# Two 256-column matmuls in place of a 512-column one in the weight-stationary products, and two feature tiles in a PSUM bank

## The chip, the cores and the metric

The kernel runs on one core of one Trainium2 chip. The metric is the device time of the program in microseconds, the median of the timed runs. The profile is one execution, taken by the hardware profiler on that core.

## The reference

A two-layer trunk over 256 tokens of width 2048, all in float32. Layer 0 is gated linear attention and a squared-ReLU MLP, layer 1 is stick-breaking attention over one shared K/V and another such MLP. Cut to what matters here:

```
h = x                                              # (256, 2048)
h = h + gla_mixer(rms_norm(h), ...)                # proj = x @ w_in: q, k (1024 each), v, r (2048 each), a_low (16)
h = h + sq_relu_mlp(rms_norm(h), w_up0, w_down0)   # square(relu(x @ w_up)) @ w_down, 2048 -> 8192 -> 2048
k, v = rms_norm(h) @ kv_w                          # 512 each
h = h + stick_breaking(rms_norm(h) @ w_q, k, v) @ w_out
h = h + sq_relu_mlp(rms_norm(h), w_up1, w_down1)
return rms_norm(h)
```

Every product with a weight matrix is kept close to float32 accuracy by splitting both sides in a high part and a rest (both float32r) and adding three partial products: high by high, rest of the tokens by high weights, high tokens by the rest of the weights.

## The kernel before, in words

**Weights.** `plan` lists all weight units of 1 MB in the order of use. `prefetch` loads one unit into `raw` (pool `wraw`, three buffers, issued from SP) and splits it half by half: ScalarE casts the high part `wh` (L147), VectorE takes the difference `wl` (L148), both into pool `wsp`, three buffers of each. `next_half` keeps three halves ready. A half holds eight k tiles of 128x128 for a weight-stationary product.

**Two forms of product.** Token-stationary products (`half_n`, L202 to L204: the down projections `dn`, `op`, `v`, `r`, `sv`) hold 128 tokens still and move 512 weight columns. Each is three matmuls of 512 columns, with stationaries that are slices of an activation tile (`hT`, `oT`, `xg`, `xkv`). Weight-stationary products (`unit_t`, L160 to L182: `up`, `qk`, `sk`, `sq`, `alow`) hold a 128x128 block of weights still and move the tokens. An activation tile has, for each of the 16 k tiles, 512 columns: 256 high and 256 rest, side by side. For each k tile (a block, below) `unit_t` issues two matmuls into one bank of pool `psB` (two banks): L169 moves all 512 columns against `wh`, so that high by high lands in columns 0 to 255 and rest by high in columns 256 to 511, and L172 moves the 256 high columns against `wl` into columns 0 to 255. The low one stands ahead of the high one, but for the first k tile.

**Finishing a unit.** `joined` (L185 to L188) copies columns 256 to 511 of the bank to SBUF on ScalarE and adds them to the others on VectorE. The MLP then takes the squared ReLU on VectorE (L562), and splits the result into `hT`: ScalarE the high part (L563), VectorE the rest (L564). All that is 256 columns wide.

**Order.** The MLP goes through four quarters of the 8192 features: 16 `up` units, then four column chunks of `dn` over the same features. `hT` is in pool `actp` for the quarters 0 and 2 and in `actc` for 1 and 3 (L556). Engines take their instructions in program order. Attention work (scores, outputs) stands in generators and is handed out by `pump` after every half of a product, so that its small matmuls lie between the blocks.

Of the kernel before, what the change touches and what calls it, by code (L numbers as in the profile page):

```python
# [8 lines left out]
F32 = mybir.dt.float32  # L9
# [4 lines left out]
ALU = mybir.AluOpType  # L14
# [25 lines left out]
def yoco_kernel(ctx: ExitStack, tc: tile.TileContext, a: dict):  # L40
    nc = tc.nc
    V, S, PE = nc.vector, nc.scalar, nc.tensor

    # one table set serves every function used here
    S.preload_act_table_set("natural_log_exp_and_others")
# [23 lines left out]

# [1 line left out]
    pending = []  # L71
# [10 lines left out]

    # the first n given out so far have to be complete
    def drain(n=None):
# [6 lines left out]

    # ---- weights: every unit is loaded whole, then split in halves, exactly, into a
    # 12-bit part and the rest; splits are issued ahead of the products that use them ----
    def out_order(w):
# [27 lines left out]
    def prefetch():  # L122
        i = state["n"]
        if i == 2 * len(plan):
            return
        state["n"] += 1
        if i % 2 == 0:
            for todo in before.pop(i // 2, []):
                todo()
            raw = wraw.tile([P, 2048], F32, tag="raw", name="raw")  # L130
            for lo, hi in ((0, 512), (512, 1024), (1024, 2048)) if i == 0 else ((0, 2048),):
                nc.sync.dma_start(raw[:, lo:hi], plan[i // 2][:, lo:hi])
                for todo in between.pop((i, hi), []):
                    todo()
            state["raw"] = raw
        part = state["raw"][:, (i % 2) * 1024:(i % 2 + 1) * 1024]
        last = i - 2 * len(plan) + 8
        if last < 0:
            wh = wsp.tile([P, 1024], F32R, tag="wh", name="wh")
            wl = wsp.tile([P, 1024], F32R, tag="wl", name="wl")  # L140
        else:
            # the last chunk's products come one token tile after the other: all its weights stay
            if last == 0:
                state["stay"] = [act_tile(n).rearrange("p k t -> p (k t)") for n in ("stay_h", "stay_l")]
            wh, wl = [b[:, last * 1024:(last + 1) * 1024] for b in state["stay"]]
        for lo, hi in ((0, 512), (512, 1024)) if i == 0 else ((0, 1024),):
            S.copy(wh[:, lo:hi], part[:, lo:hi])  # L147
            V.tensor_tensor(wl[:, lo:hi], part[:, lo:hi], wh[:, lo:hi].bitcast(F32), op=ALU.subtract)  # L148
        ready.append((wh, wl))
# [8 lines left out]

    # out[feature, token]: weights stationary, [high | low] tokens moving
    def unit_t(act, name, steps=1):  # L160
        ps = psB.tile([P, 512], F32, tag="psB", name=name)
        for kt in range(KT):
            if kt % 8 == 0:
                wh, wl = next_half()
            o = (kt % 8) * P
            first, last = kt == 0, kt == KT - 1

            def high():
                PE.matmul(ps, wh[:, o:o + P], act[:, kt, :], start=first, stop=last)  # L169

            def low():
                PE.matmul(ps[:, 0:T], wl[:, o:o + P], act[:, kt, 0:T], start=False, stop=False)  # L172

            if first:
                high()
                low()
            else:
                low()
                high()
            if kt % 8 == 7:  # L180
                pump(steps)
        return ps  # L182

    # sum of the two halves of a bank
    def joined(ps, out, rows=P):  # L185
        lo = t256("lo")
        S.copy(lo[0:rows], ps[0:rows, T:2 * T])  # L187
        V.tensor_tensor(out, ps[0:rows, 0:T], lo[0:rows], op=ALU.add)  # L188

    # out[token, column chunk]: tokens stationary, weights moving  # L190
    def banks(name):
# [24 lines left out]

    # a tile as the sum of two that the tensor engine takes in one pass
    def split(src, tile):
# [12 lines left out]

    # 1 / sqrt(u), one Newton step behind the tables
    def rsqrt(u, out):
# [9 lines left out]

# [1 line left out]
    ident = const.tile([P, P], F32, name="ident")  # L245
# [20 lines left out]

# [1 line left out]
    xg = act_tile("xg")  # L268
# [48 lines left out]

    # a value per token, from partitions to the free axis of all partitions
    def spread(col, out, scale):
# [6 lines left out]

    # transposed, scaled and split: what the next products read
    def feed(c, targets):
# [29 lines left out]

# [1 line left out]
    oT = act_tile("oT")  # L360

    # scores of one head: decayed queries and keys, level by level; every exponent is at most 0
    def scores(hd, qT, kT, st, sx):
# [21 lines left out]

        # between the two token tiles, and on the diagonal
        e = t512("e0").rearrange("p (f t) -> p f t", f=2)
# [19 lines left out]

        # within them: keys of a pair's first half against queries of its second
        for lv, s in enumerate(LEVELS):
# [30 lines left out]

    # outputs of one head, its norm, the gate
    def outputs(hd, st, sx, vv, gs):
# [42 lines left out]

    # the output gate times the head's gain
    def gates(pss):
# [14 lines left out]
    def queries_keys():  # L502
        qT = g512("qk", 4, "qT").rearrange("p (f t) -> p f t", f=2)
        kT = g512("qk", 4, "kT").rearrange("p (f t) -> p f t", f=2)
        for dst in (qT, kT):
            for f in range(2):
                joined(unit_t(xg, "qk"), dst[:, f])
        return qT, kT

    for hd in range(GLA_H):  # L510
        st = [half.tile([P, P], F32, tag=f"st{t}", name=f"st{t}", bufs=1) for t in range(NT)]
        sx = half.tile([P, P], F32, tag="sx", name="sx", bufs=1)
        if hd == 0:
            pv, pr = banks("v"), banks("r")
            for kg in range(4):
                unit_n(pv, xg, kg)
                unit_n(pr, xg, kg)
            qT, kT = queries_keys()
            drain()
            vv = values(pv)  # L520
            gs = gates(pr)
            araw = t256("araw")
            spread(rstd0, rbc0, 1.0)
            joined(unit_t(xg, "alow"), araw[0:16], rows=16)
            V.tensor_tensor(alow, araw[0:16], rbc0[0:16], op=ALU.mult)
            give(scores(hd, qT, kT, st, sx))
        else:
            qT, kT = queries_keys()
            give(scores(hd, qT, kT, st, sx))
            vv = values(chunk_n(xg, "v"))  # L530
            gs = gates(chunk_n(xg, "r"))
# [22 lines left out]
    def mlp(act, rstd2, ssq, after, last=None):  # L554
        for q in range(NQ):
            hT = act_tile("hT", actc if q % 2 else actp)  # L556
            for f in range(KT):
                ps = unit_t(act, "up")
                s = t256("s")
                joined(ps, s)  # L560
                y = t256("y")
                V.scalar_tensor_tensor(y, s, 0.0, s, op0=ALU.max, op1=ALU.mult)  # L562
                S.copy(hT[:, f, 0:T], y)  # L563
                V.tensor_tensor(hT[:, f, T:2 * T], y, hT[:, f, 0:T].bitcast(F32), op=ALU.subtract)  # L564
            for c in range(NCH):
# [39 lines left out]

# [1 line left out]
    rstd, _ = squared_rstd(ssq, "rstd2")  # L607
# [3 lines left out]
    kvs = const.tile([P, 2048], F32, tag="kvs", name="kvs")  # L611
    for n in range(KVH):
        joined(unit_t(xkv, "sk"), kvs[:, n * T:(n + 1) * T])
    ps = chunk_n(xkv, "sv")
# [19 lines left out]

    # one group of heads; keys on partitions, (head, query) along the free axis
    def sticks(n, qs):
        heads = slice(n * GRP, (n + 1) * GRP)

        # scores of a key tile against a query tile
        def score(qt, kt):  # L640
# [11 lines left out]

        # softplus, split: the products below have a side of ones and zeros
        def soft(z):
# [7 lines left out]

        # less everything between the key (itself too) and the query
        def weigh(z, own, later=None):
# [45 lines left out]
    for n in range(KVH):  # L710
        qs = [t512(f"q{t}") for t in range(NT)]
        for g in range(GRP):
            ps = unit_t(xq, "sq", 1 + (len(pending) > 1 or g == GRP - 1))
            s = t256("s")
            joined(ps, s)
            for t in range(NT):
                V.tensor_tensor(qs[t][:, g * P:(g + 1) * P], s[:, t * P:(t + 1) * P],
                                rbc[:, t * P:(t + 1) * P], op=ALU.mult)
        give(sticks(n, qs))
# [45 lines left out]

# ---- layouts: stationary units [feature tile][partition][k tile, 128], moving units
# [1 line left out]
def _stationary(w):  # L768
# [17 lines left out]
def _lay_out(i):  # L786
# [27 lines left out]
    r["final_g"] = np.ascontiguousarray(i["final_g"])  # L814
    # constants of the shapes alone
    r["ident"] = np.eye(P, dtype=np.float32)
# [27 lines left out]
```

## Time and profile before

| what | value |
|---|---|
| device time, median of 3 runs | 2115.25 us (2115.14 to 2115.3) |
| profiled execution, first to last instruction | 2113.3 us |
| TensorE matmul busy | 2097.4 us, 99% of the span |
| weight loads on TensorE | 1763.1 us, 83% |
| VectorE busy | 1313.0 us, 62% |
| ScalarE busy | 1039.5 us, 49% |
| DMA read | 384.58 MB, 183 GB/s over the span |

The profile gives no other time of its own execution than the span; the runs are some 2 us longer than it. A matmul's row has a start that is recorded and an end that is modelled, so durations of consecutive matmuls overlap; how long one holds the engine is read from start to start. A weight load (PEld) belongs to each matmul and runs beside the matmul ahead of it.

### The profile page before, as it was taken

Reading aid. Unit: us, or ns where it says so; the run is one execution under the profiler, and the core shown is the slowest. Engines: PE = TensorE matmul, PEld = TensorE weight load, DVE = VectorE, ACT = ScalarE, POOL = GpSimd, SP = SyncE. Lnnn points to the kernel's source line nnn. Section 1 sums busy time; section 2 is a strip of 40 time slices with the busy share of each in tenths; the row PEclk is TensorE's granted clock in tenths of the full one; section 3 lists DMA queues with packets and bytes.
Section 4 is the critical chain, followed back from the end, with each engine's and each line's share of the span. In section 5 each row is a group of like instructions: output and inputs, shape, how many; then the busy total and the mean of one; then the engine's idle time right before and its main releaser. Section 6 shows DMA issues by size and latency. Waiting matters only on the chain.

```text
span 2113.3 us, 26650 instructions
## 1 busy us (share of the span) xinstructions
PE 2097.4 (99%) x10544; PEld 1763.1 (83%) x10544; DVE 1313.0 (62%) x1804; ACT 1039.5 (49%) x1447; POOL 0.2 (0%) x4
## 2 busy tenths in 40 slices
PE   8999999999999999999999999999999999999998
PEld 7888888888888888888888888888888888888886
DVE  5767876665566556556666687666556546655655
ACT  5645655544344344434455487544344434434443
POOL 0000000000000000000000000000000000000000
PEclk9999999999999999999999999999999999999999
DMA  8544444555555555555555644455555555555553
GB/s 313 180 160 160 156 164 157 182 180 188 192 194 183 188 191 181 197 189 190 182 182 178 216 142 156 165 188 188 193 187 190 187 186 192 181 197 185 193 182 137
DMA packets 55741, 388.40 MB, mean 184 GB/s; under 512 B 6448, under 2 KB 6960, under 8 KB 9152
## 3 DMA queue, kind: packets, MB, share of 16 engines
q1 hardware_dynamic: 55616, 386.70, 53.3%
q8 instruction: 83, 1.36, 0.3%
q14 instruction: 42, 0.34, 0.0%
HBM read 384.58 MB, written 2.10 MB: 183 GB/s over the span
## 4 chain that ended last, share of the span: by engine, by line
PE 98%; DVE 0%; ACT 0%; DMA 0%; SPq 0%; issue 0%; DVEq 0%
PE up L169 23%; PE up L172 11%; PE dn L204 11%; PE dn L203 11%; PE dn L202 11%; PE sq L169 3%; PE op L204 3%; PE op L202 3%; PE op L203 3%; PE qk L169 3%; PE sq L172 1%; PE r L202 1%; PE r L204 1%; PE r L203 1%; PE v L204 1%; PE v L202 1%
## 5 line engine op out<-in xcount | busy, mean ns | idle before, releaser
L148 DVE TENSOR_TENSOR wl<-raw,wh 128x1024 fp32r<-128x1024 f32 (+1 forms) x715 | 874.6, 1224 | 593.2 <-ACT wh L147 580.7
L147 ACT CAST wh<-raw 128x1024 fp32r<-128x1024 f32 (+1 forms) x715 | 751.2, 1051 | 725.9 <-PE dn L203 392.0
L169 PE MATMUL up<-xm,wh 128*128 128x512 f32 x2048 | 714.7, 398 | 0.0
L172 PE MATMUL up<-xm,wl 128*128 128x256 f32 x2048 | 554.5, 281 | 0.0
L169 PEld LDWEIGHTS up<-xm,wh 128*128 128x128 f32 x2048 | 376.8, 188 | 84.0
L172 PEld LDWEIGHTS up<-xm,wl 128*128 128x128 f32 x2048 | 386.8, 189 | 10.8
L204 PE MATMUL dn<-wl,hT 128*128 128x512 f32 x992 | 390.3, 393 | 0.0
L203 PE MATMUL dn<-wh,hT 128*128 128x512 f32 x992 | 389.0, 392 | 0.0
L202 PE MATMUL dn<-wh,hT 128*128 128x512 f32 x992 | 387.5, 391 | 0.0
L203 PEld LDWEIGHTS dn<-wh,hT 128*128 128x128 f32 x992 | 186.2, 188 | 42.6
L202 PEld LDWEIGHTS dn<-wh,hT 128*128 128x128 f32 x992 | 186.2, 188 | 41.3
L204 PEld LDWEIGHTS dn<-wl,hT 128*128 128x128 f32 x992 | 186.2, 188 | 40.8
L187 ACT COPY lo<-up 128x256 f32<-128x256 f32 x128 | 47.7, 373 | 227.6 <-PE up L169 227.6
L188 DVE TENSOR_TENSOR s<-up,lo 128x256 f32<-128x256 f32 x128 | 54.4, 425 | 118.4 <-ACT lo L187 118.4
L202 PE MATMUL op<-wh,oT 128*128 128x512 f32 x256 | 101.1, 395 | 0.0
L203 PE MATMUL op<-wh,oT 128*128 128x512 f32 x256 | 101.0, 395 | 0.0
L204 PE MATMUL op<-wl,oT 128*128 128x512 f32 x256 | 100.7, 394 | 0.0
L169 PE MATMUL sq<-xq,wh 128*128 128x512 f32 x256 | 91.0, 396 | 0.0
L169 PE MATMUL qk<-xg,wh 128*128 128x512 f32 x256 | 90.5, 397 | 0.0
L172 PE MATMUL qk<-xg,wl 128*128 128x256 f32 x256 | 69.9, 283 | 0.0
L172 PE MATMUL sq<-xq,wl 128*128 128x256 f32 x256 | 69.4, 280 | 0.0
L202 PE MATMUL v<-wh,xg 128*128 128x512 f32 x128 | 51.7, 404 | 6.3 <-ACT wh L147 6.3
(206 smaller groups left out, 1838.2 us busy)
## 6 DMA issues: line engine op xcount, KB each, us to landing
raw<-in_w_up SPq DMA_DIRECT2D x128, 1024.0 KB, 4.9
raw<-in_w_down SPq DMA_DIRECT2D x128, 1024.0 KB, 4.9
raw<-in_w_r SPq DMA_DIRECT2D x16, 1024.0 KB, 4.9
raw<-in_w_out SPq DMA_DIRECT2D x16, 1024.0 KB, 4.8
raw<-in_w_sq SPq DMA_DIRECT2D x16, 1024.0 KB, 4.8
raw<-in_w_so SPq DMA_DIRECT2D x16, 1024.0 KB, 5.0
raw<-in_w_v SPq DMA_DIRECT2D x15, 1024.0 KB, 4.9
raw<-in_w_q SPq DMA_DIRECT2D x8, 1024.0 KB, 4.9
```

The source lines that it names most:

```text
L147: S.copy(wh[:, lo:hi], part[:, lo:hi])
L148: V.tensor_tensor(wl[:, lo:hi], part[:, lo:hi], wh[:, lo:hi].bitcast(F32), op=ALU.subtract)
L169: PE.matmul(ps, wh[:, o:o + P], act[:, kt, :], start=first, stop=last)
L172: PE.matmul(ps[:, 0:T], wl[:, o:o + P], act[:, kt, 0:T], start=False, stop=False)
L187: S.copy(lo[0:rows], ps[0:rows, T:2 * T])
L188: V.tensor_tensor(out, ps[0:rows, 0:T], lo[0:rows], op=ALU.add)
L202: PE.matmul(pss[t], xl, wh[:, o:o + CH], start=kt == 0, stop=False)
L203: PE.matmul(pss[t], xh, wh[:, o:o + CH], start=False, stop=False)
L204: PE.matmul(pss[t], xh, wl[:, o:o + CH], start=False, stop=kt == KT - 1)
```

## The change

A helper `pair_t` replaces `unit_t` and `joined`. For a block it issues three matmuls of 256 columns into the same 256 columns of a bank: high tokens against `wh`, rest tokens against `wh`, high tokens against `wl`. The second half of the bank takes the next feature tile, so two units fill one bank. What is finished is then 512 columns wide, read straight from PSUM: in the MLP a ReLU on ScalarE, its product with the sums on VectorE, the square of the ReLU on ScalarE as the high part, and the rest on VectorE.

```diff
-    def unit_t(act, name, steps=1):
+    def pair_t(act, name, steps=(1, 1), count=2):
         ps = psB.tile([P, 512], F32, tag="psB", name=name)
-        for kt in range(KT):
-            if kt % 8 == 0:
-                wh, wl = next_half()
-            o = (kt % 8) * P
-            first, last = kt == 0, kt == KT - 1
-            def high():
-                PE.matmul(ps, wh[:, o:o + P], act[:, kt, :], start=first, stop=last)
-            def low():
-                PE.matmul(ps[:, 0:T], wl[:, o:o + P], act[:, kt, 0:T], start=False, stop=False)
-            if first:
-                high()
-                low()
-            else:
-                low()
-                high()
-            if kt % 8 == 7:
-                pump(steps)
+        for j in range(count):
+            out = ps[:, j * T:(j + 1) * T]
+            for kt in range(KT):
+                if kt % 8 == 0:
+                    wh, wl = next_half()
+                o = (kt % 8) * P
+                PE.matmul(out, wh[:, o:o + P], act[:, kt, 0:T], start=kt == 0, stop=False)
+                PE.matmul(out, wh[:, o:o + P], act[:, kt, T:2 * T], start=False, stop=False)
+                PE.matmul(out, wl[:, o:o + P], act[:, kt, 0:T], start=False, stop=kt == KT - 1)
+                if kt % 8 == 7:
+                    pump(steps[j])
         return ps
...
-    def joined(ps, out, rows=P):
-        lo = t256("lo")
-        S.copy(lo[0:rows], ps[0:rows, T:2 * T])
-        V.tensor_tensor(out, ps[0:rows, 0:T], lo[0:rows], op=ALU.add)
...
         for dst in (qT, kT):
-            for f in range(2):
-                joined(unit_t(xg, "qk"), dst[:, f])
+            S.copy(dst, pair_t(xg, "qk").rearrange("p (f t) -> p f t", f=2))
...
-            for f in range(KT):
-                ps = unit_t(act, "up")
-                s = t256("s")
-                joined(ps, s)
-                y = t256("y")
-                V.scalar_tensor_tensor(y, s, 0.0, s, op0=ALU.max, op1=ALU.mult)
-                S.copy(hT[:, f, 0:T], y)
-                V.tensor_tensor(hT[:, f, T:2 * T], y, hT[:, f, 0:T].bitcast(F32), op=ALU.subtract)
+            for f in range(0, KT, 2):
+                ps = pair_t(act, "up")
+                s, y = t512("s"), t512("y")
+                S.activation(s, ps, AF.Relu)
+                V.tensor_tensor(y, s, ps, op=ALU.mult)
+                sv, yv = [b.rearrange("p (f t) -> p f t", f=2) for b in (s, y)]
+                S.activation(hT[:, f:f + 2, 0:T], sv, AF.Square)
+                V.tensor_tensor(hT[:, f:f + 2, T:2 * T], yv, hT[:, f:f + 2, 0:T].bitcast(F32), op=ALU.subtract)
```

`sk` and `sq` take pairs in the same way; `alow` takes one unit, half a bank.

On TensorE, where the first MLP's second quarter begins, the rows were these (`dn` is the down projection, `up` the unit in its bank, `xm` the tokens):

```order
2650 L204 MATMUL dn_4888<-wl,hT 128x512
2651 L169 MATMUL up<-xm,wh 128x512
2652 L172 MATMUL up<-xm,wl 128x256 x2
2653 L169 MATMUL up<-xm,wh 128x512
2654 L172 MATMUL up<-xm,wl 128x256
2655 L169 MATMUL up<-xm,wh 128x512
```

and in the changed program, within such a quarter, they are these:

```order
3633 L169 MATMUL up<-xm,wh 128x256
3634 L170 MATMUL up<-xm,wh 128x256
3635 L171 MATMUL up<-xm,wl 128x256
3636 L169 MATMUL up<-xm,wh 128x256
3637 L170 MATMUL up<-xm,wh 128x256
3638 L171 MATMUL up<-xm,wl 128x256
```

A block has become three matmuls, each with its own stationary, instead of two; the columns moved, 768 a block, are the same.

On ScalarE, at the start of the first MLP, casts of weights (L147) stood one by one between the two steps that finish a unit (L187 and L563):

```order
257 L147 CAST wh<-raw 128x1024
258 L187 COPY lo<-up 128x256
259 L147 CAST wh<-raw 128x1024
260 L563 CAST hT<-y 128x256
261 L147 CAST wh<-raw 128x1024
262 L187 COPY lo<-up 128x256
```

and now four of them stand between one pair's finish and the next one's:

```order
247 L147 CAST wh<-raw 128x1024 x4
248 L543 ACTIVATE s<-up 128x512
249 L546 ACTIVATE hT<-s 128x2x256
250 L147 CAST wh<-raw 128x1024 x4
251 L543 ACTIVATE s<-up 128x512
```

The finish has moved together: both ScalarE steps follow each other, once for two units, and the first of them waits for the last matmul of the pair.

## Rows read from the trace of the kernel before

**Rows 1.** The page: span, busy time by engine, granted TensorE clock in 40 slices.

```profile
span 2113.3 us, 26650 instructions
PE 2097.4 (99%) x10544; PEld 1763.1 (83%) x10544; DVE 1313.0 (62%) x1804; ACT 1039.5 (49%) x1447; POOL 0.2 (0%) x4
PEclk9999999999999999999999999999999999999999
```

**Rows 2.** Waits of TensorE's matmuls: total us, times, longest.

```profile
PE v L202 <- ACT wh L147: 6.3, 1, 6.3
```

**Rows 3.** Groups by line on TensorE, the 512-column weight-stationary matmuls: count, busy, modelled ns.

```profile
L169 PE MATMUL up<-xm,wh 128*128 128x512 f32 x2048 | 714.7, 398 | 0.0
...
L169 PE MATMUL sq<-xq,wh 128*128 128x512 f32 x256 | 91.0, 396 | 0.0
L169 PE MATMUL qk<-xg,wh 128*128 128x512 f32 x256 | 90.5, 397 | 0.0
...
L169 PE MATMUL sk<-xkv,wh 128*128 128x512 f32 x64 | 22.9, 401 | 0.0
...
L169 PE MATMUL alow<-xg,wh 128*128 128x512 f32 x16 | 5.7, 392 | 0.0
```

**Rows 4.** Timeline of TensorE, three blocks of `up`: start us, modelled us.

```profile
805.97 0.40 PE L169 MATMUL up<-xm,wh 128*128 128x512 f32 x1
806.20 0.28 PE L172 MATMUL up<-xm,wl 128*128 128x256 f32 x1
806.32 0.40 PE L169 MATMUL up<-xm,wh 128*128 128x512 f32 x1
806.55 0.28 PE L172 MATMUL up<-xm,wl 128*128 128x256 f32 x1
806.66 0.40 PE L169 MATMUL up<-xm,wh 128*128 128x512 f32 x1
806.91 0.28 PE L172 MATMUL up<-xm,wl 128*128 128x256 f32 x1
807.03 0.40 PE L169 MATMUL up<-xm,wh 128*128 128x512 f32 x1
```

**Rows 5.** Timeline of TensorE, quarter 0's `dn`: 58 rows, first and last.

```profile
559.99 0.39 PE L202 MATMUL dn<-wh,hT 128*128 128x512 f32 x1
...
572.91 0.39 PE L202 MATMUL dn<-wh,hT 128*128 128x512 f32 x1
```

**Rows 6.** Timeline of TensorE, quarter 1's `dn`: 58 rows, first and last.

```profile
699.66 0.39 PE L202 MATMUL dn<-wh,hT 128*128 128x512 f32 x1
...
712.96 0.39 PE L202 MATMUL dn<-wh,hT 128*128 128x512 f32 x1
```

**Rows 7.** Timeline of TensorE, four blocks of `sq`, first row and first of the next.

```profile
1262.18 0.40 PE L169 MATMUL sq<-xq,wh 128*128 128x512 f32 x1
...
1263.57 0.40 PE L169 MATMUL sq<-xq,wh 128*128 128x512 f32 x1
```

**Rows 8.** Timeline of TensorE, where one `up` unit ends and the next begins.

```profile
810.21 0.62 PE L169 MATMUL up<-xm,wh 128*128 128x512 f32 x2
810.67 0.40 PE L172 MATMUL up<-xm,wl 128*128 128x256 f32 x2
810.90 0.40 PE L169 MATMUL up<-xm,wh 128*128 128x512 f32 x1
```

**Rows 9.** Timeline of TensorE, short matmuls one after the other, each with its own stationary.

```profile
96.17 1.05 PE L401 MATMUL cross<-qT,kT 128*128 128x128 f32 x8
97.06 0.61 PE L401 MATMUL cross<-e 128*128 128x128 f32 x4
```

**Rows 10.** Groups by line, weight loads of matmuls that repeat the stationary `upper`.

```profile
L667 PEld LDWEIGHTS tail<-lo,upper 128*128 128x128 f32 x12 | 2.3, 188 | 0.6
```

**Rows 11.** Groups by line on ScalarE and VectorE: 512-column operations as the change adds them.

```profile
L672 ACT ACTIVATE z<-z 128x512 f32<-128x512 f32 x12 | 7.6, 631 | 4.3 <-DVE z L671 4.0
...
L671 DVE TENSOR_TENSOR z<-z,tail 128x512 f32<-128x512 f32 x12 | 8.2, 684 | 4.5 <-PE tail L667 3.8 <-PE tail L670 0.7
```

More of the change, by code (lines that the diff above doesn't have):

```diff
@@ L521, in yoco_kernel @@
             gs = gates(pr)
-            araw = t256("araw")
             spread(rstd0, rbc0, 1.0)
-            joined(unit_t(xg, "alow"), araw[0:16], rows=16)
-            V.tensor_tensor(alow, araw[0:16], rbc0[0:16], op=ALU.mult)
+            V.tensor_tensor(alow, pair_t(xg, "alow", count=1)[0:16, 0:T], rbc0[0:16], op=ALU.mult)
             give(scores(hd, qT, kT, st, sx))
@@ L611, in yoco_kernel @@
     kvs = const.tile([P, 2048], F32, tag="kvs", name="kvs")
-    for n in range(KVH):
-        joined(unit_t(xkv, "sk"), kvs[:, n * T:(n + 1) * T])
+    for n in range(0, KVH, 2):
+        S.copy(kvs[:, n * T:(n + 2) * T], pair_t(xkv, "sk"))
     ps = chunk_n(xkv, "sv")
@@ L711, in yoco_kernel @@
         qs = [t512(f"q{t}") for t in range(NT)]
[L712 to L715, printed above, removed]
+        for g in range(0, GRP, 2):
+            ps = pair_t(xq, "sq", [1 + (len(pending) > 1 or g + j == GRP - 1) for j in range(2)])
+            pv = ps.rearrange("p (g t q) -> p g t q", g=2, t=NT)
             for t in range(NT):
-                V.tensor_tensor(qs[t][:, g * P:(g + 1) * P], s[:, t * P:(t + 1) * P],
-                                rbc[:, t * P:(t + 1) * P], op=ALU.mult)
+                V.tensor_tensor(qs[t][:, g * P:(g + 2) * P].rearrange("p (g q) -> p g q", g=2), pv[:, :, t],
+                                rbc[:, t * P:(t + 1) * P].rearrange("p (o q) -> p o q", o=1).broadcast_to([P, 2, P]),
+                                op=ALU.mult)
         give(sticks(n, qs))
```

## The prediction

> **What bounds the kernel now.** I began with the page: TensorE is busy 2097.4 of the 2113.3 us span, and the granted clock is at its upper level, 2.4 GHz, in every slice [rows 1]. A busy row alone proves little, since the ends of matmuls are modelled, so I looked at the waits: TensorE waited once for a cast at the start, 6.3 us, and for almost nothing afterwards [rows 2]. ScalarE and VectorE have 51% and 38% of the span free [rows 1]. So the time is the sum over the matmuls of the time from one start to the next, and the question is what a block (one k tile of a weight-stationary unit) takes as two matmuls and as three. Everything else has to be shown to stay hidden.
>
> There are 2048 blocks in `up`, 256 in `sq`, 256 in `qk`, 64 in `sk` and 16 in `alow`: 2640 [rows 3]. Three blocks of `up` take 807.03 - 805.97 = 1.06 us, so 0.3533 us each [rows 4]. Four of `sq` take 1.39 us, 0.3475 each [rows 7]. For the 592 blocks outside `up` I take 0.350, the middle of the two.
>
> **What a matmul costs besides its columns.** The moved columns do not change: 512 + 256 before, 3 x 256 after, 768 a block. What changes is the count of matmuls and of weight loads, 2 to 3. So I need the price of one more matmul at equal columns. No row of before has three 256-column matmuls in sequence, so it must come from the nearest ones.
>
> The two down projections separate the terms. In quarter 0 a 512-column matmul takes (572.91 - 559.99) / 57 = 0.2267 us [rows 5]; in quarter 1 the same instruction takes (712.96 - 699.66) / 57 = 0.2333 us [rows 6]. The code differs only in the pool that holds the stationary `hT` (L556). So there is a cost per matmul of 0.0067 us that depends on where the stationary lies, beside 0.2267 / 512 = 0.443 ns a column. Applied to `up`, whose stationaries lie in a third pool, `wsp`: 768 x 0.443 ns + 2 x 0.0067 = 0.3400 + 0.0133 = 0.3533 us. That is what three blocks show to the last digit [rows 4], so I take stationaries in `wsp` to cost 0.0067 each, whatever the number of columns behind them.
>
> With three matmuls a block is then 0.3400 + 3 x 0.0067 = 0.3600 us.
>
> The bounds. Below: if a 256-column matmul cost its columns alone, 3 x 0.1133 = 0.340. Above: the longest interval of a 512-column matmul beside its load is 0.25 us (806.66 to 806.91) [rows 4], 10% over 0.2267; three of 256 columns with that surcharge are 0.375. Between them are rows that read the 256-column matmul itself. In the alternation its three intervals to the next start are 0.12, 0.11 and 0.12 us [rows 4], a mean of 0.1167, so 0.350 for three. At a unit's end two of them follow each other and take 0.23 us together, 0.115 each [rows 8], so 0.345. These speak for less than I take. I still take 0.360, because a start may be early or late by what its neighbours lost: only sums over a repeating pattern are free of that, and the sums over `dn` and over whole `up` blocks give the same 0.0067 per matmul.
>
> The Trainium skill (TensorE: Matmul & The Clock Gate, section "Back-to-back issue gap") gives the isolated gap as columns over 2.4 GHz plus about 2.5 ns, a fixed cost per matmul of the same kind. By it a block goes from 325.0 to 327.5 ns, and 2640 of them add 6.6 us. The trace agrees on a fixed cost but not on its size: quarter 1's `dn` is 233 ns where the rule has 216.
>
> **Do the loads bind?** A block now needs three weight loads. Their rows last 0.188 us each [rows 10], which would be 0.564 us a block if they could not overlap. But eight short matmuls, each with its own load, start every (97.06 - 96.17) / 8 = 0.111 us [rows 9]; three are 0.333 us, below even 0.340. So a load takes 0.111 in a row of loads, and fits behind a 256-column matmul, with only 2% to spare at the lower bound. Repeating `wh` does not save a load: the second matmul against the same `upper` has one of its own, all 12 times [rows 10].
>
> **What else moves, and what hides it.** Finishing a pair takes, by 512-column operations of the same kind, 0.63 us for the ReLU, 0.68 for the product from PSUM, 0.63 for the square, 0.68 for the rest: 2.6 us in sequence [rows 11]. I cost it at nothing. The bank is read for 1.3 us, and the pair after it fills the other bank for 32 x 0.36 = 11.5 us. The ReLU now waits for 32 blocks instead of 16, and the next casts of `wh` queue behind it on ScalarE; but two halves are split ahead, 2 x 8 x 0.36 = 5.8 us of products. After a quarter's last pair, `dn` reads the last two feature tiles only in its last half of eight, after 7 x 12 x 0.2267 = 19 us. If one of these covers failed, it would be about 2.6 us at eight quarter ends, 21 us; I see nothing for it. The work taken from ScalarE and VectorE is off the path and gives nothing back. `qk` now delivers queries in one copy at the end of a pair, but the first step that uses them stands behind other products. No DMA is added or moved.
>
> **The sum.** `up`: 2048 x (0.3600 - 0.3533) = 13.7 us. The rest: 592 x (0.3600 - 0.3500) = 5.9 us. Together 19.6 us on a span of 2113.3, with the 2 us around it unchanged: 2115.25 + 19.6 = 2135 us, 0.9% slower.
>
> **Rivals.**
> - *Grouped 256-column matmuls are cheap (faster).* The cost may lie in changing between 512 and 256 columns, and fall when all are alike. For it: the pair at 0.115 us [rows 8] and the mean of 0.1167 [rows 4]. Against it: quarter 1's `dn` has equal matmuls throughout and pays [rows 6]. It decides where a 256-column matmul takes less than 0.3533 / 3 = 0.1178 us. At 0.116: `up` 2048 x (0.348 - 0.3533) = -10.9, the rest 592 x -0.002 = -1.2, so 2103 us. At the lower bound: 2048 x -0.0133 + 592 x -0.010 = -33, so 2082 us. Chance 0.28.
> - *It cancels.* A matmul at 0.1175 to 0.118 leaves the time within 4 us. Chance 0.10.
> - *A smaller fixed cost.* `sq` pays (0.3475 - 0.3400) / 2 = 0.0037 per matmul [rows 7], so a third matmul could cost that everywhere: 2640 x 0.0037 = 9.8, so 2125 us. Against it: the 0.0067 is the rule in `up`, which has most of the blocks [rows 4]. Chance 0.07. The gap rule of the Trainium skill named above (TensorE: Matmul & The Clock Gate) is this rival with a size of its own, and gives 2122 us.
> - *The loads collide.* Three loads in 0.36 us use TensorE's load path for 0.333 of it; if each matmul then pays the 10% above, a block is 0.375: 2048 x 0.0217 + 592 x 0.025 = 59, so 2174 us. For it: the load rate and the column rate are nearly equal. Against it: the short matmuls run at the load rate without loss [rows 9]. Chance 0.10.
>
> My forecast, 0.1200 us a matmul, has 0.45.
>
> **How the numbers follow.** 0.2% of the time, 4 us, is about what a measurement of this kernel can tell from no change. Slower: 0.45 + 0.07 + 0.10 = 0.62; the same: 0.10; faster: 0.28. The forecast's own range is 2127 to 2142 us (0.1190 to 0.1210 a matmul). The full range has to take in the faster case down to 0.1145 a matmul, 2090 us, and reaches up to 2145; it leaves out colliding loads (0.10) and the cheapest end of the faster case (0.08).
>
> **What would show it.** In the timeline of `up`, three matmuls from one L169 to the next should take 0.360 us on average over many blocks; 0.340 to 0.350 means the faster rival, 0.375 the colliding loads. The `dn` stages should be as they were, 0.2267 and 0.2333 by turns. TensorE's waits should remain at the one of 6.3 us; a wait of L169 for `psB` or of L202 for `hT` would show a cover failed. ScalarE's and VectorE's busy time should fall without effect. I am wrong if the price per matmul was not a price per matmul, but one of the alternation.

## The result and the profile after

| | before | after |
|---|---|---|
| device time, median of 4 runs each, same chip | 2115.19 us (2115.11 to 2115.3) | 2138.95 us (2138.07 to 2139.45) |
| ratio | | 1.0112, 95% interval 1.0097 to 1.0127 |
| profiled execution | 2113.3 us | 2136.3 us |

The kernel became 23.8 us slower, 1.1%. The forecast was 2135 us, so the direction, the size and the range were right. One of its reasons was not, as the experiments show.

The page of the changed kernel, to be read beside [rows 1]:

```profile
span 2136.3 us, 31482 instructions
...
PE 2118.9 (99%) x13184; PEld 1906.3 (89%) x13184; DVE 1229.2 (58%) x1495; ACT 1018.1 (48%) x1292; POOL 0.2 (0%) x4
...
PEclk9999999999999999999999999999999999999999
```

There are 2640 more matmuls and as many more weight loads, one of each per block. VectorE lost 84 us of work and ScalarE 21, and neither gave anything back. The granted clock is at its upper level throughout, so it has no part in the difference.

TensorE's longest two waits in the changed kernel (total us, times, longest), beside [rows 2]:

```profile
PE v L188 <- ACT wh L147: 6.3, 1, 6.3
PE sk L170 <- DVE xkv L327: 1.2, 1, 1.2
```

The wait at the start is the old one. The second row is new: in `sk` a matmul of rest tokens waits for VectorE to write the rest part of a tile of `xkv`. VectorE begins that write 6.6 us after the first matmul of `sk` in both kernels, so it has not become later; TensorE now reaches the matmul that needs it 1.2 us too early. Three further waits last 0.3 to 0.5 us each. There is no wait for `hT` and none for a bank.

The timeline of TensorE in the first MLP's third quarter, beside [rows 4]:

```profile
819.82 0.28 PE L169 MATMUL up<-xm,wh 128*128 128x256 f32 x1
819.94 0.28 PE L170 MATMUL up<-xm,wh 128*128 128x256 f32 x1
820.06 0.28 PE L171 MATMUL up<-xm,wl 128*128 128x256 f32 x1
820.18 0.28 PE L169 MATMUL up<-xm,wh 128*128 128x256 f32 x1
...
820.90 0.28 PE L169 MATMUL up<-xm,wh 128*128 128x256 f32 x1
```

The starts stand 0.120 us apart, and three blocks from 819.82 to 820.90 take 1.08 us: 0.3600 each, where it was 0.3533. Busy time by engine over that quarter and the `dn` stage behind it (PE, PEld, DVE, ACT, POOL, then granted clock, DMA share, GB/s):

```profile
783.11:875.26 92.15, 92.15 (x770) 92.14 (x769) 49.20 (x48) 41.40 (x46) 0.00 (x0) 1.00 0.51 183
875.26:962.32 87.06, 87.06 (x386) 72.08 (x385) 45.09 (x41) 34.91 (x35) 0.00 (x0) 1.00 0.55 193
```

In `up` the row of some weight load covers every moment (92.14 of 92.15 us); in `dn` it is so for 72.08 of 87.06. A load's row lasts 0.19 us, longer than the 0.120 from one to the next, so full cover does not by itself show that the loads are the limit.

Where the 23.0 us between the two spans lie, from the first matmul of each stage to the first of the next, in us:

| stages | before | after | difference |
|---|---|---|---|
| `up`, eight quarters | 724.3 | 739.1 | +14.8 |
| `sq` | 105.5 | 109.5 | +3.9 |
| `qk`, four stages | 106.6 | 109.1 | +2.6 |
| `sk` | 24.0 | 25.9 | +1.8 |
| `dn`, quarters 0 and 1 of the first MLP | 87.04, 89.60 | 87.07, 89.60 | under 0.1 |

Of the other stages, the first `v` is 0.3 us longer and layer 1's out projection 0.4 shorter; the rest agree within 0.1 us.

### The profile page after: what moved, and what is told of

It reads as the page before. It is cut to its first block, busy times and chain, and to the rows that moved or that the text cites. A ratio compares the mean times of both kernels' runs of the same rounds, so it can differ in the third digit from the quotient of the medians.

```text
span 2136.3 us, 31482 instructions
## 1 busy us (share of the span) xinstructions
PE 2118.9 (99%) x13184; PEld 1906.3 (89%) x13184; DVE 1229.2 (58%) x1495; ACT 1018.1 (48%) x1292; POOL 0.2 (0%) x4
## 4 chain that ended last, share of the span: by engine, by line
PE 98%; DVE 1%; ACT 1%; DMA 0%; issue 0%; SPq 0%; DVEq 0%
PE up L171 12%; PE up L170 12%; PE up L169 12%; PE dn L189 11%; PE dn L188 11%; PE dn L190 11%; PE op L190 3%; PE op L189 3%; PE op L188 3%; PE sq L169 1%; PE r L188 1%; PE sq L170 1%; PE sq L171 1%; PE r L190 1%; PE qk L169 1%; PE r L189 1%
## 5 line engine op out<-in xcount | busy, mean ns | idle before, releaser
L147 ACT CAST wh<-raw 128x1024 fp32r<-128x1024 f32 (+1 forms) x715 | 749.0, 1048 | 1029.1 <-PE up L170 400.9
L171 PE MATMUL up<-xm,wl 128*128 128x256 f32 x2048 | 579.8, 283 | 0.0
L169 PE MATMUL up<-xm,wh 128*128 128x256 f32 x2048 | 579.8, 283 | 0.0
L170 PE MATMUL up<-xm,wh 128*128 128x256 f32 x2048 | 579.6, 283 | 0.0
L169 PEld LDWEIGHTS up<-xm,wh 128*128 128x128 f32 x2048 | 393.2, 192 | 0.3
L170 PEld LDWEIGHTS up<-xm,wh 128*128 128x128 f32 x2048 | 393.2, 192 | 0.3
L171 PEld LDWEIGHTS up<-xm,wl 128*128 128x128 f32 x2048 | 393.2, 192 | 0.0
L169 PE MATMUL qk<-xg,wh 128*128 128x256 f32 x256 | 73.2, 286 | 0.0
L169 PE MATMUL sq<-xq,wh 128*128 128x256 f32 x256 | 72.4, 283 | 0.3 <-DVE q L699 0.3
L170 PE MATMUL qk<-xg,wh 128*128 128x256 f32 x256 | 72.5, 283 | 0.0
```

The lines of the kernel that those rows point to most:

```text
L169: PE.matmul(out, wh[:, o:o + P], act[:, kt, 0:T], start=kt == 0, stop=False)
L170: PE.matmul(out, wh[:, o:o + P], act[:, kt, T:2 * T], start=False, stop=False)
L171: PE.matmul(out, wl[:, o:o + P], act[:, kt, 0:T], start=False, stop=kt == KT - 1)
```

## The experiments

The kernel before was run again on the same chip beside each group of runs; its medians there were between 2114.94 and 2115.49 us. Three questions were asked in turn: is the loss in the matmuls or in the finish, does the price depend on where the stationary lies, and does it come from the loads or on top of the columns.

### The finish taken back: e3_three_matmuls_unit_finish

The changed kernel, with one unit per bank and a finish 256 columns wide in the MLP:

```diff
-            for f in range(0, KT, 2):
-                ps = pair_t(act, "up")
-                s, y = t512("s"), t512("y")
+            for f in range(KT):
+                ps = pair_t(act, "up", count=1)[:, 0:T]
+                s, y = t512("s")[:, 0:T], t512("y")[:, 0:T]
...
```

> The changed kernel, but the MLP takes one unit per PSUM bank and finishes it 256 columns wide, so that of the change in the MLP only the three matmuls a block are left. If the finish is hidden, as predicted: 2139 us within 2 us, blocks at 0.360, no new wait of TensorE. If the wide finish of pairs cost part of the 24 us: towards 2135 us or less. If it gave part of a larger loss back: 2145 us or more.

It took 2138.28 us (2138.19 to 2138.32), ratio 1.0105 (1.009 to 1.012), and every `up` quarter is within 0.02 us of the changed kernel's. The pairing in a bank and the wide finish change nothing that can be measured in the MLP, so there the three matmuls are the whole loss. (`qk`, `sk` and `sq` still take pairs in this kernel.)

### The weights' pool moved: e1_after_weights_low and e2_before_weights_low

Pool `wsp`, which holds the stationaries of `up`, is opened ahead of the activations' pool and so lies below it in SBUF. The edit is the same in both kernels:

```diff
+    wsp = ctx.enter_context(tc.tile_pool(name="wsp", bufs=3))
     actp = ...
...
-    wsp = ctx.enter_context(tc.tile_pool(name="wsp", bufs=3))
```

> The changed kernel with one edit: the pool of the split weights, wsp, is opened ahead of the activation pool, so that wh and wl lie where the first activation buffers lay. Surcharge theory (each matmul pays 0.0067 us for a stationary in wsp's old place, none in the new one): a block goes from 0.360 to 0.340 us, so 2139 - 2640 x 0.020 = 2086 us. Load theory (a weight load beside a full-rate matmul takes 0.120 us wherever it is read, and sets the pace): blocks stay at 0.360, 2139 us.

> The kernel before with the same edit of the pool order. Surcharge theory: a block goes from 0.3533 to 0.340 in up and from 0.350 to 0.340 elsewhere, 2048 x 0.0133 + 592 x 0.010 = 33 us less, 2082 us; the two forms of block then cost the same and this kernel and the changed one with low weights end within 5 us of each other. Load theory: the loads of two matmuls a block were hidden, so nothing changes, 2115 us.

The changed kernel took 2138.26 us (ratio 1.0105, 1.009 to 1.012) and the kernel before 2115.24 (ratio 0.9998, 0.9988 to 1.0008). The timeline of `up` in the changed kernel with moved weights:

```profile
820.03 0.28 PE L169 MATMUL up<-xm,wh 128*128 128x256 f32 x1
...
821.11 0.28 PE L169 MATMUL up<-xm,wh 128*128 128x256 f32 x1
```

Three blocks again take 1.08 us, and both times are those of the load theory: the surcharge by place falls. So the price is not one of the place as such. The edit left one thing as it was: the distance in SBUF between the weight tiles and `xm` was a multiple of 4096 bytes before it and is one after it.

### The loads laid bare: e4_narrow_two_of_three

The changed kernel, in which two of the three matmuls of a block move only 128 columns; the correction products of the last 128 tokens are left out:

```diff
-                PE.matmul(out, wh[:, o:o + P], act[:, kt, T:2 * T], ...)
-                PE.matmul(out, wl[:, o:o + P], act[:, kt, 0:T], ...)
+                PE.matmul(out[:, 0:P], wh[:, o:o + P], act[:, kt, T:T + P], ...)
+                PE.matmul(out[:, 0:P], wl[:, o:o + P], act[:, kt, 0:P], ...)
```

> The changed kernel with two of the three matmuls of a block cut to 128 columns: the correction products of the last 128 tokens are left out. Surcharge theory without a floor: a block is 0.1200 + 2 x (0.0567 + 0.0067) = 0.247 us. If loads bind at the pace of the short matmuls of before, 0.111: 0.120 + 2 x 0.111 = 0.343, or less if a load can start under the wide matmul. If a load takes 0.120: 0.360, and the narrower matmuls save nothing.

Its time, 2154.3 us (one run), cannot be compared: the granted clock fell to its lower level, 1.2 GHz, for stretches of `qk`, `sk` and `sq`. The clock on the page comes first. The windows below it (busy us of PE, PEld, DVE, ACT and POOL, then granted clock, DMA share, GB/s) are the last `qk` before and after the fall, and 1150 to 1320 us, from `sk` into `sq`:

```profile
PEclk9999879999999999999997998999999999999999
```

```profile
243.70:252.30 8.60, 6.31 (x56) 6.20 (x56) 8.60 (x16) 7.16 (x12) 0.00 (x0) 1.00 0.17 70
252.40:296.70 44.30, 44.17 (x198) 43.04 (x198) 16.55 (x40) 11.09 (x15) 0.00 (x0) 0.50 0.26 96
1150.00:1320.00 170.00, 159.94 (x1018) 149.42 (x1017) 93.77 (x122) 86.47 (x124) 0.00 (x0) 0.85 0.41 143
```

Before the fall TensorE had been busy for only 6.31 of 8.60 us. In `up` the clock stayed at its upper level, so that stage can be read. Weight loads there:

```profile
630.01 0.19 PEld L171 LDWEIGHTS up<-xm,wl 128*128 128x128 f32 x1
630.12 0.19 PEld L169 LDWEIGHTS up<-xm,wh 128*128 128x128 f32 x1
630.23 0.19 PEld L170 LDWEIGHTS up<-xm,wh 128*128 128x128 f32 x1
630.35 0.19 PEld L171 LDWEIGHTS up<-xm,wl 128*128 128x128 f32 x1
630.46 0.19 PEld L169 LDWEIGHTS up<-xm,wh 128*128 128x128 f32 x1
630.57 0.19 PEld L170 LDWEIGHTS up<-xm,wh 128*128 128x128 f32 x1
630.69 0.19 PEld L171 LDWEIGHTS up<-xm,wl 128*128 128x128 f32 x1
```

Two blocks take 0.68 us, 0.340 each, although a block now moves only 512 columns, 0.227 us by the pace of [rows 5]. Here the loads set the pace. A load beside a 128-column matmul is followed by the next after 0.11 us, one beside the 256-column matmul after 0.12. So with one 256-column matmul in it, a block of three loads did not get below 0.34 us, few as its columns are. The 0.111 of [rows 9] held. But the changed kernel's 0.360 is 0.020 above that, and this run does not say whether a load beside a full stream takes 0.120 or the columns take 0.0067 more.

### Wider matmuls: w1_wide_272

This was to tell those two apart. The kernel with the finish taken back moves 272 columns in place of 256 in `up`, and discards the other 16:

```diff
+                n = T + 16 if name == "up" else T
...
+                m = n if kt < KT - 1 else T
-                PE.matmul(out, wh[:, o:o + P], act[:, kt, 0:T], ...)
-                PE.matmul(out, wh[:, o:o + P], act[:, kt, T:2 * T], ...)
-                PE.matmul(out, wl[:, o:o + P], act[:, kt, 0:T], ...)
+                PE.matmul(out, wh[:, o:o + P], flat[:, a:a + n], ...)
+                PE.matmul(ps[:, j * T:j * T + m], wh[:, o:o + P], flat[:, b:b + m], ...)
+                PE.matmul(out, wl[:, o:o + P], flat[:, a:a + n], ...)
```

> The changed kernel with one unit per PSUM bank, in which each matmul of the up products moves 272 columns in place of 256 (the last k tile's second matmul keeps 256); the 16 extra columns are discarded. Theory that the weight load sets the pace (a load takes 0.120 us beside a full stream, and 272 columns at 0.2267/512 = 0.443 ns are 0.1204 us): a block of up stays at 0.360 to 0.362 us, a quarter of up near 92.2, 2138 to 2143 us in all. Theory of a fixed surcharge of 0.0067 us on the columns: 3 x (0.1204 + 0.0067) = 0.381 us a block, 2,048 x 0.021 = 43 us more, near 2182 us.

It took 2170.93 us (one run), 32.7 us above the kernel with the finish taken back. Its timeline:

```profile
819.99 0.28 PE L174 MATMUL up<-xm,wh 128*128 128x272 f32 x1
820.11 0.29 PE L175 MATMUL up<-xm,wh 128*128 128x272 f32 x1
820.24 0.29 PE L176 MATMUL up<-xm,wl 128*128 128x272 f32 x1
820.36 0.28 PE L174 MATMUL up<-xm,wh 128*128 128x272 f32 x1
...
820.74 0.29 PE L174 MATMUL up<-xm,wh 128*128 128x272 f32 x1
```

Six intervals take 0.75 us, 0.125 each; by the whole quarter (96.21 us for 256 blocks) a block takes 0.3758. A load that takes 0.120 whatever it stands beside would have left 0.36 to 0.362: that theory falls. The time follows the columns, but not fully. Sixteen columns are worth 16 x 0.443 = 7.1 ns a matmul, and 5.3 ns came. The price on top of the columns fell from 6.7 ns to about 5. So neither theory holds as it was stated. The fixed price is the nearer one, and it is not quite fixed. That a load takes longer the more columns stream beside it would fit both this run and the one before it, and was not tested.

### The distance between two tiles: p1_before_others_shift, p2_before_actc_shift, s1_before_actc_distance

If not the place, what separates quarter 0's `dn` [rows 5] from quarter 1's [rows 6]? Both stream the same weight tiles past `hT`; what differs is the distance in SBUF from those tiles to `hT`. As allocated, the first `wh` lies 90,112 bytes above the `hT` of `actp`, a multiple of 4096, and the `hT` of `actc` lies 57,248 bytes above that `wh`, 96 short of a multiple; all six weight buffers are multiples of 4096 apart. Three kernels, each the kernel before with unused bytes ahead of a pool, here the third:

```diff
+    padp = ctx.enter_context(tc.tile_pool(name="padp", bufs=1))
+    pad2 = padp.tile([P, 24], F32, name="pad2")
+    V.memset(pad2, 0.0)
```

The 24 words are 96 bytes. The second has 8 words (32 bytes) there. The first has 32 bytes at the bottom of SBUF, which moves everything and leaves all distances.

> The kernel before with 32 unused bytes in the constant pool, so that all tiles behind it start on a multiple of 64 bytes and actc now does not. If what counts is the moved tile (a row of 256 columns that is not on a 64-byte boundary touches 17 pieces of 64 bytes instead of 16): 512 columns fall from 0.2267 to about 0.2135 us and 256 columns from 0.1133 to 0.1067 in every stage, near 2005 us. If only equal or unequal alignment of the two counts: dn of quarters 1 and 3 stays at 0.2333, 2115 us.

> The kernel before with 32 unused bytes ahead of the pool actc alone. In the kernel before all activation and weight tiles start 32 bytes past a multiple of 64, but actc starts on one; hT of quarters 1 and 3 and oT2 lie there. Alignment theory (a stationary that starts otherwise within 64 bytes than the moved tile costs 0.0067 us a matmul): dn of quarters 1 and 3 goes from 0.2333 to 0.2267 us a matmul and the last out projection too, 4 x 2.56 + 768/2 x 0.0067 = 13 us less, 2102 us; up keeps 0.3533. If the place of actc matters and not the alignment: no change, 2115 us.

> The kernel before with 96 unused bytes ahead of pool actc, so that its hT buffer lies a multiple of 4,096 bytes from the weight tiles that the down products move, as the buffer in actp does. Theory of distance: the down products of quarters 1 and 3 take 0.2267 us a matmul like those of quarters 0 and 2, 4 x 2.56 us less, and the out projection of layer 1 some 2 to 3 us less: near 2102 us. If the distance has no such part and any shift gives what 32 bytes gave (0.2289 us a matmul): near 2107 us. Theory that the buffer's pool decides: 2115 us.

| kernel | `hT` of `actc` to a multiple of 4096 | a matmul of quarter 1's `dn` | device time |
|---|---|---|---|
| before | 96 bytes short | 0.2333 us | 2115.3 us |
| everything shifted by 32 | 96 short | 0.2333 | 2115.5 (one run) |
| `actc` shifted by 32 | 64 short | 0.2288 | 2107.35 (one run) |
| `actc` shifted by 96 | 0 | 0.2267 | 2103.59 (2103.21 to 2105.59), ratio 0.9944 (0.9931 to 0.9958) |

The rows of quarter 1's `dn` with `actc` shifted by 32 bytes, first and last of 58:

```profile
699.64 0.39 PE L202 MATMUL dn<-wh,hT 128*128 128x512 f32 x1
...
712.68 0.39 PE L202 MATMUL dn<-wh,hT 128*128 128x512 f32 x1
```

and with it shifted by 96:

```profile
699.47 0.39 PE L202 MATMUL dn<-wh,hT 128*128 128x512 f32 x1
...
712.39 0.39 PE L202 MATMUL dn<-wh,hT 128*128 128x512 f32 x1
```

The 57 intervals take 13.04 and 12.92 us, where they took 13.30 in [rows 6]. In the last kernel the four odd `dn` stages lose 10.1 us and the out projection of layer 1, whose stationary lies in `actc` too, 1.9: together 12.0, and the medians differ by 11.7. No instruction of TensorE was changed. In the second and third row of the table `actc` starts at the same address, and only its distance to the weights differs. So the price in `dn` is set by the distance between the tile that streams and the tile that is loaded, and at a multiple of 4096 the pace is quarter 0's. The theory of equal alignment, which had 0.2267 for the shift by 32 bytes, falls: that shift took two thirds of the price. The kernel with 96 bytes is also faster than both kernels of this study.

### Both kernels with the 32 bytes in both places: p3_before_all_aligned and q3_after_all_aligned

> The kernel before with both paddings: every tile, actc too, starts on a multiple of 64 bytes. Moved-tile theory: 512 columns at 0.2135 us in all dn, 4704 x 0.013 = 61 us less, and blocks of two matmuls at 0.320 to 0.327, 2640 x 0.030 = 79 us less, together near 1980 us. Relative theory: dn at 0.2267 throughout, 2102 us. Surcharge by place or history: no change, 2115 us.

> The changed kernel with both paddings. Moved-tile theory: a 256-column matmul needs 0.107 us for its columns, less than the 0.110 to 0.111 at which loads follow each other, so a block is 3 x 0.111 = 0.333 us and the loss against the padded kernel before shrinks to 2640 x 0.010 = 26 us or less, near 2005 us. If the 0.120 is the pace of loads beside a moved stream whatever its alignment: blocks stay at 0.360, and only dn gains, near 2075 us. Surcharge by place or history: 2139 us.

They took 2106.94 us (ratio 0.9962, 0.9948 to 0.9976) and 2130.02 (ratio 1.0071, 1.0056 to 1.0086). Both gain in `dn`, whose quarter 1 takes 87.89 us in each, and not in `up` (90.34 and 92.15 us). No theory named these times: the padding leaves `actc` 64 bytes short of a multiple, and 87.89 us is also what the shift of `actc` alone by 32 bytes gives. That the moved tile starts on a multiple of 64 bytes is worth nothing. The change costs 23.1 us here as well, so its loss does not hang on that of `dn`.

### Six different distances: r1_after_weights_staggered and r2_before_weights_staggered

Each buffer of `wh` and `wl` is 96 bytes longer, so that the six lie at different distances from everything else; the same edit in both kernels:

```diff
-            wh = wsp.tile([P, 1024], F32R, tag="wh", name="wh")
-            wl = wsp.tile([P, 1024], F32R, tag="wl", name="wl")
+            wh = wsp.tile([P, 1048], F32R, tag="wh", name="wh")[:, 0:1024]
+            wl = wsp.tile([P, 1048], F32R, tag="wl", name="wl")[:, 0:1024]
```

> The changed kernel with each buffer of wh and wl 96 bytes longer, so that the six buffers begin at six different distances (multiples of 32 bytes) from the tokens; halves of eight k tiles take them in turn. Distance theory (loads and moved columns get in each other's way by the distance of their addresses): the interval of the 256-column matmuls differs from half to half, from 0.113 to 0.127 us, by the buffer that is being loaded. Load-pace theory (a load beside a stream of 256-column matmuls takes 0.120 us): 0.120 in every half, 2139 us within the change in dn.

> The kernel before with the same edit. Distance theory: blocks of up differ from half to half between 0.340 and 0.367 us, and dn between 0.2267 and 0.2333 by the buffer that moves. Load-pace theory: the blocks keep 0.3533 in every half, since loads of two matmuls have slack; only dn varies.

One run each: 2134.93 us for the changed kernel and 2120.92 for the one before, 14.0 us apart instead of 23.8. The timeline of `up` in the changed one:

```profile
819.77 0.28 PE L169 MATMUL up<-xm,wh 128*128 128x256 f32 x1
...
820.83 0.28 PE L169 MATMUL up<-xm,wh 128*128 128x256 f32 x1
```

Three blocks take 1.06 us in this half. By a whole quarter a block takes 90.59 / 256 = 0.3539 us (0.3600 in the changed kernel), and in the kernel before 89.57 / 256 = 0.3499 (0.3529). The halves do differ, but only from 0.353 to 0.356 us a block, much less than the distance theory had; the load-pace theory, 0.120 everywhere, falls. So the distance matters in `up` too, but there the multiple of 4096 is not the good case, and no distance that was tried comes near 0.340, the columns at the best pace of `dn`.

In the kernel before, the `dn` of the even quarters lose by the edit (89.4 us against 87.04 in quarter 0) and those of the odd ones gain less (88.9 against 89.60). That is why it gets slower. The buffers show within a stage. In quarter 1's `dn` these are the first matmuls of four halves, and of the half after them:

```profile
701.46 0.40 PE L202 MATMUL dn<-wh,hT 128*128 128x512 f32 x1
...
704.27 0.39 PE L202 MATMUL dn<-wh,hT 128*128 128x512 f32 x1
...
707.02 0.39 PE L202 MATMUL dn<-wh,hT 128*128 128x512 f32 x1
...
709.79 0.40 PE L202 MATMUL dn<-wh,hT 128*128 128x512 f32 x1
...
712.60 0.39 PE L202 MATMUL dn<-wh,hT 128*128 128x512 f32 x1
```

The halves take 2.81, 2.75, 2.77 and again 2.81 us for 12 matmuls each: the pace repeats with the three buffers, while `hT` and the instructions stay the same.

## Why the prediction was right, and where it was not

- **What bounds the kernel**: right. The sum over matmul starts is the time; 84 us less on VectorE moved nothing.
- **The price of a matmul in `up`**: right in size. Forecast 0.3600 us a block, found 0.3600; 13.7 us forecast for `up`, 14.8 found. The difference is for the most part that a block of before takes 0.3529 over a whole quarter, a little less than the 0.3533 read from three blocks. That the size came out so well is partly luck, as the next point shows.
- **"Depends on where the stationary lies"**: this step failed. Moving the pool did nothing in either kernel, and moving `actc` by 96 bytes, past the same pools and in the same order, removed the price from `dn`. What counts there is the distance between two tiles. In `up` the distance changes the price but does not remove it. That 0.0067 came out alike in `dn` and in `up` was partly chance: in `dn` it belongs to 96 bytes short of a multiple of 4096, in `up` to the multiple itself. Nor is the distance all in `up`. In the kernel before, at one and the same distance, the first two units of the first MLP's third quarter run at different paces. These are the second and the last high matmul of each:

```profile
777.12 0.40 PE L169 MATMUL up<-xm,wh 128*128 128x512 f32 x1
...
781.97 0.63 PE L169 MATMUL up<-xm,wh 128*128 128x512 f32 x2
...
782.67 0.40 PE L169 MATMUL up<-xm,wh 128*128 128x512 f32 x1
...
787.62 0.62 PE L169 MATMUL up<-xm,wh 128*128 128x512 f32 x2
```

Fourteen blocks take 4.85 us in the first unit and 4.95 in the second, 0.346 and 0.354 us each. So a pace near the 0.3475 of [rows 7] occurs in `up` too, and the 0.3533 of [rows 4] holds for most of its blocks, not for all. Nothing that was run tells what decides between the two. The changed kernel has 0.3600 in half after half.
- **"Whatever the number of columns behind them"**: nearly. The price over the columns was 6.7 ns at 256 and about 5 at 272.
- **The bounds and the loads**: the lower bound of 0.340 was rightly no place to land, for a second reason that I gave only 2% of room: three loads alone take 0.340 when two of the matmuls are cut to 128 columns. Whether at 256 columns the loads or the columns set the 0.120 is not shown.
- **The other 592 blocks**: right in price, but two terms were left out. Forecast 5.9 us, found 8.3. `qk` came out as forecast (2.6). `sq` gave 3.9 instead of 2.6. Added up from start to start, its own matmuls grew by 2.5 us (89.8 to 92.3); the other 1.4 lie in the attention matmuls between them (15.7 to 17.1), of which one has come over from the out projection behind. `sk` gave 1.8 instead of 0.6, of which 1.2 us are the new wait for `xkv`; I had written that TensorE's waits should stay at one.
- **The finish, the casts, `hT`**: right, they cost nothing; taking the finish back gave no time. Its four operations last 0.59, 0.68, 0.63 and 0.69 us, as [rows 11] let expect:

```profile
L546 ACT ACTIVATE hT<-s 128x512 fp32r<-128x512 f32 x64 | 40.5, 633 | 2.0
L543 ACT ACTIVATE s<-up 128x512 f32<-128x512 f32 x64 | 38.0, 594 | 0.0
...
L547 DVE TENSOR_TENSOR hT<-y,hT 128x512 fp32r<-128x512 f32 x64 | 44.3, 692 | 6.7
L544 DVE TENSOR_TENSOR y<-s,up 128x512 f32<-128x512 f32 x64 | 43.5, 680 | 0.0
```

- **The rivals**: cheap grouped matmuls would have needed 0.1178 or less; they take 0.1200 in half after half. The smaller fixed cost, read from `sq`, did not come, since `sq` now takes 0.120 a matmul as well. The colliding loads (0.375 a block) did not come either. The short intervals of [rows 4] and [rows 8] did not carry over; that a neighbour had their loss fits, but was not tested.

The estimate from the fixed 2.5 ns of the Trainium skill (TensorE: Matmul & The Clock Gate, section "Back-to-back issue gap") was 6.6 us for the added matmuls. The trace does not agree: the stages that hold them grew by 23.1 us, of which 1.2 are the wait.

What stays open: why a 256-column matmul in the changed `up` costs 4.3 to 6.7 ns above its columns at every distance that was tried, why the blocks of before have two paces at one distance, and why 16 more columns cost only three quarters of their pace. A scan of the distance in `up` alone, with `dn` left as it is, was not run, nor the changed kernel with the 96 bytes.

## What to carry to other kernels

On a TensorE-bound kernel, count matmuls as well as columns: splitting a 512-column matmul in two adds a weight load and a price of some nanoseconds, here 0.0071 us a block of 0.3529, and work saved on engines that have time to spare does not pay for it. Read a price per matmul from sums over a repeating pattern, not from single intervals, which give one matmul's loss to the next. Where the same instruction is slower in one stage than in another, compare the SBUF distance of its two operands early; in `dn` and the out projection here 96 unused bytes were worth 0.56% of the kernel, while in `up` the distance was only part of it.

## What the runs showed of the hardware that was not expected

- The pace of a stream of 512-column matmuls with a load beside each depends on the distance between the streamed tile and the loaded one: 0.2267 us at a multiple of 4096 bytes, 0.2288 at 64 bytes short of it, 0.2333 at 96 short. A shift of both tiles together does nothing: 0.2333 before and after it. The Trainium skill (TensorE: Matmul & The Clock Gate, section "Step-by-step: what each phase is for") says that loading the next weights takes no read bandwidth from the running matmul. The trace does not agree for these float32r matmuls: the same `dn` gained 2.9% by the distance alone.
- Beside 128-column matmuls a weight load started 0.11 us after the one before it, beside a 256-column one 0.12. In the kernel with narrow matmuls three loads held a block at 0.340 us, where the columns need 0.227.
- With two of three matmuls cut to 128 columns, the granted clock fell to its lower level in `qk` (0.50 from 252.40 to 296.70 us), while TensorE was busy for 44.17 of these 44.30 us; just before, at the upper level, it had been busy for 6.31 of 8.60. In `up`, with the same narrow matmuls and no wait, it did not fall.
